# One trunk layer on one core: SSD states by a running scan, and one more pair of blocks by seven products

## The chip, the cores and the metric

The kernel runs on 1 core of one Trainium2 chip. The metric is device microseconds of one execution (us); lower is better. Each time is the median of several runs, and one more execution is profiled. In the profile PE is TensorE's matmuls, PEld its weight loads, DVE is VectorE, ACT ScalarE, POOL GpSimd, and SP the engine that issues most DMAs.

## The reference, cut to what matters

One layer of a hybrid trunk handles 1024 prompt tokens and 8 samples of 16 tokens with shared weights, all in fp32. Chunk-band attention and a Mamba-2 SSD branch share one input projection, and are gated, merged and projected. The change touches the projection's order and the SSD state recurrence:

```python
proj = h @ w_in        # q | k | v | z_att | z_ssd | x,B,C | dt | two merge gates
# per chunk, per SSD head (32 heads of 64 columns, state of 128):
h_new = h * exp(a_cs[:, -1]) + einsum('blgn,blgep->bgepn', bk, xdt * to_end)   # state after the chunk
y_st  = einsum('blgn,bgepn->blgep', ck, h) * exp(a_cs)                         # what the state adds to y
```

The kernel works the prompt in 8 chunks of 128 tokens. State after chunk c = decay(c) times the state after chunk c-1, plus the product of B and the weighted x of chunk c.

## The kernel before, in words

Activations are kept transposed: 128 channels on the partitions, 1152 tokens along the columns. Weights and activations are split into a high and a low part, and each product is three matmuls in fp32r: high by high, high by low, low by high (lines 489, 490, 492). A *block* is 128 output channels of the projection: 8 contraction steps, 3 groups of 384 tokens, 3 matmuls, so 72 matmuls of 384 columns.

The program goes through five stages. (1) The input is loaded and normalised. (2) *Blocks ahead*: the silu gates z of the SSD branch and some merge gates are computed and put into DRAM, the first of them plainly; then NPR *pairs* of blocks are computed together by Strassen's scheme with seven products in the place of eight (`pairs`, lines 880 to 883: 7 forms, 4 contraction steps, 2 halves, 3 matmuls, so 168 matmuls of 288 columns per pair); then one more block plainly. (3) Attention, eight head pairs. (4) The *SSD stage*: 16 head pairs p, in 4 groups. Each pair has a dense part (`conv_gen`, one block, and where `FILL` names the pair a *filler*, which is one further block of z or gate which does not depend on the head pair) and a light part (`prelude` and `main`, many small matmuls with work on DVE, ACT and POOL). (5) The tail: merge gates left over, two branch projections, the output projection.

In `main` of a head pair: x is turned to tokens on the partitions (L1754) and written in two weighted copies, xd and xw (L1758). Eight 128x128 matmuls give B times xw, chunk by chunk, into two PSUM tiles `g` of four chunks (L1799; fp32 matmuls stand as two records each in the trace). ACT copies chunk 0 into `hst` (L1804), and DVE makes the other states in turn, two heads for each of seven chunks (L1808, 14 instructions of 64 columns). Then PE makes the part inside the chunk (L1830), the samples' part (L1837) and the states' part (L1855, which reads `hst` as its weights); DVE adds them up. PSUM has four `g` tiles, two `d`, and one `s` of two banks.

The order in which instructions stand is made by generators and a scheduler: a planner keeps its own clock, adds each generator step's cost, and `pause(t)` holds a generator until the planner's clock has moved t ns. The scheduler then places instructions on each engine, which executes them in that order.

Of the kernel before, what the change touches and what calls it, by code (L numbers as in the profile page):

```python
# [12 lines left out]
P = 128  # L13
# [18 lines left out]
NEARLY = 15  # L32
SLOTS = (('p', 1), ('p', 3), ('p', 6), ('p', 9), ('p', 11), ('p', 13), ('p', 15))
# [5 lines left out]
NPR = 7  # L39
# [92 lines left out]
def trunk_kernel(ctx: ExitStack, tc: tile.TileContext, h):  # L132
# [118 lines left out]
    L_SSD = marena.set_layout(Z0, [("X", 1, XW), ("R", 2, 1184), ("t", 8, 36), ("pad", 1, 576), ("T", 9, NT), ("Y", 1, 1184), ("H", 1, 1024),  # L251
# [1294 lines left out]
    def dt_gen():  # L1546
# [36 lines left out]
        nc.scalar.activation(dec, pe[:, :256], AF.Exp)  # L1583
# [101 lines left out]
    def ssd(p):  # L1685
# [7 lines left out]
        e4 = dec.rearrange("p (c e) -> p c e", e=32)  # L1693
# [43 lines left out]
        def main():  # L1737
# [46 lines left out]
            def masked(q):  # L1784

                t = alloc(L_ST, "x", 2 * P)
                i = 2 * (q % 2)
                nc.gpsimd.tensor_tensor(t.r.rearrange("p (b n) -> p b n", n=P), xs[q // 2].ap.unsqueeze(1).to_broadcast([P, 2, P]),
                                        bmask4[:, i:i + 2].unsqueeze(2).to_broadcast([P, 2, P]), ALU.mult)
                return t  # L1790

            xm = [masked(0), masked(1)]

            yield from pause(1500)
            for j in range(2):
                ps = pg()
                for s in range(4):
                    c = 4 * j + s
                    nc.tensor.matmul(ps[:, s * P:(s + 1) * P], tokb.ap[:, c * P:(c + 1) * P], xw.ap[:, c * P:(c + 1) * P],  # L1799
                                     start=True, stop=True)  # L1800
                for s in range(4):
                    c = 4 * j + s
                    if c == 0:
                        nc.scalar.activation(hst.ap[:, 0:P], ps[:, 0:P], AF.Copy)  # L1804
                        continue
                    for e in range(2):
                        o = c * P + e * HD
                        nc.vector.scalar_tensor_tensor(  # L1808
                            hst.ap[:, o:o + HD], hst.ap[:, o - P:o - P + HD], e4[:, c, 2 * p + e:2 * p + e + 1],
                            ps[:, s * P + e * HD:s * P + e * HD + HD], ALU.mult, ALU.add)  # L1810
                yield 4 * 213
                yield from pause(900)
            xw.free()
# [4 lines left out]
            yield from pause(1200)  # L1818
# [395 lines left out]
```

## Time and profile before

| what | value |
|---|---|
| median of 3 runs | 1942.8 us (1938.79 to 1944.55) |
| the profiled execution | 1943.42 us |
| its span, first to last instruction | 1941.6 us |
| granted TensorE clock | 0.999 |
| busy: PE, DVE, ACT, POOL | 1922.7, 1251.5, 798.3, 339.7 us |
| instructions | 35765 |
| pairs by seven products | 102.2 to 258.7 us of the span |
| SSD stage, first to last of its states' matmuls | 989 to 1504 us |

A matmul's row gives how long it took from start to modelled end. Matmuls overlap in the pipeline, so the rate at which they go is the distance of their starts, and the duration in the row is longer than that. The rows of DVE overlap a little for the same reason.

### The profile page before, as it was taken

What the parts mean: (1) busy time and instruction counts of PE and PEld (TensorE: products, weight loads), DVE (VectorE), ACT (ScalarE), POOL (GpSimd) and SP (SyncE); (2) the same over time, 40 slices, a digit from 0 to 9 for tenths busy, and PEclk for the clock granted to TensorE, in tenths of its full rate; (3) what the DMA queues carried; (4) which work ended last, traced back from release to release, by engine and by line L of the source; (5) the groups of instructions that cost most, each with busy time, mean ns of one, the idle gap of its engine ahead of it and who ended that gap; (6) DMA issues with size and microseconds to landing.
All of it is one profiled execution on the core that took longest, in us unless ns stands there. A gap on an engine that the chain in (4) does not pass through costs nothing.

```text
span 1941.6 us, 35765 instructions
## 1 busy us (share of the span) xinstructions
PE 1922.7 (99%) x14259; PEld 1842.4 (95%) x14259; DVE 1251.5 (64%) x2577; ACT 798.3 (41%) x1639; POOL 339.7 (17%) x615
## 2 busy tenths in 40 slices
PE   7999999999999999999999999999999999999999
PEld 5999999999899998998999999999999999999999
DVE  6756634555556456558597988888885434777732
ACT  7533324444454444545655546465453311111200
POOL 0000003213123131221022343242241300000000
PEclk9999999999999999999999999999999999999999
DMA  8222342343333333423345354554558742331341
GB/s 316 92 81 95 109 173 69 96 129 116 97 117 101 122 116 94 130 82 115 119 132 181 132 162 152 168 173 140 160 192 289 292 144 93 105 105 56 89 143 52
DMA packets 85966, 258.73 MB, mean 133 GB/s; under 512 B 14732, under 2 KB 15768, under 8 KB 85800
## 3 DMA queue, kind: packets, MB, share of 16 engines
q1 hardware_dynamic: 77416, 229.57, 36.5%
q0 software_dynamic: 8384, 26.88, 3.6%
q8 instruction: 112, 1.84, 0.4%
q14 instruction: 54, 0.44, 0.1%
HBM read 202.72 MB, written 53.68 MB: 132 GB/s over the span
## 4 chain that ended last, share of the span: by engine, by line
PE 92%; DVE 3%; DMA 2%; ACT 1%; issue 1%; POOL 0%; SPq 0%; ACTq 0%; DVEq 0%; POOLq 0%
PE d L489 11%; PE d L492 11%; PE d L490 11%; PE d L557 5%; PE d L555 5%; PE d L556 5%; PE s L489 4%; PE s L490 4%; PE s L492 4%; PE g L1311 3%; PE g L1334 3%; PE s L1390 2%; PE g L880 2%; PE g L883 2%; PE g L882 2%; PE g L490 1%
## 5 line engine op out<-in xcount | busy, mean ns | idle before, releaser
L489 PE MATMUL d<-rarena 128*128 128x384 f32 x1288 | 437.7, 340 | 0.0
L492 PE MATMUL d<-rarena 128*128 128x384 f32 x1288 | 434.2, 337 | 0.0
L490 PE MATMUL d<-rarena 128*128 128x384 f32 x1288 | 433.3, 336 | 0.0
L489 PEld LDWEIGHTS d<-rarena 128*128 128x128 f32 x1288 | 242.0, 188 | 4.1 <-issue 2.7
L492 PEld LDWEIGHTS d<-rarena 128*128 128x128 f32 x1288 | 241.9, 188 | 2.2 <-issue 2.0
L490 PEld LDWEIGHTS d<-rarena 128*128 128x128 f32 x1288 | 242.1, 188 | 0.8 <-issue 0.4
L557 PE MATMUL d<-va_att,rarena 128*128 128x384 f32 (+1 forms) x567 | 197.6, 349 | 0.0
L555 PE MATMUL d<-va_att,rarena 128*128 128x384 f32 (+1 forms) x567 | 196.7, 347 | 0.0
L556 PE MATMUL d<-va_att,rarena 128*128 128x384 f32 (+1 forms) x567 | 193.7, 342 | 0.0
L374 ACT ACTIVATE rarena<-arena 128x1024 fp32r<-128x1024 f32 x76 | 80.5, 1059 | 262.9 <-PE s L490 173.9
L489 PE MATMUL s<-rarena 128*128 128x384 f32 x488 | 165.6, 339 | 0.0
L490 PE MATMUL s<-rarena 128*128 128x384 f32 x488 | 164.2, 336 | 0.0
L492 PE MATMUL s<-rarena 128*128 128x384 f32 x488 | 163.3, 335 | 0.0
L1299 ACT ACTIVATE ma_att<-ma_att 128x640 f32<-128x640 f32 (+2 forms) x144 | 101.5, 706 | 135.8 <-DVE ma_att L1408 99.7
L1228 POOL TENSOR_SCALAR ma_att<-ma_att 128x16 f32<-128x16 f32 (+1 forms) x24 | 5.2, 218 | 707.3 <-DVE ma_att L1205 417.2
L557 PEld LDWEIGHTS d<-va_att,rarena 128*128 128x128 f32 x567 | 107.0, 189 | 3.9 <-issue 2.7
L555 PEld LDWEIGHTS d<-va_att,rarena 128*128 128x128 f32 x567 | 106.8, 188 | 2.7 <-issue 1.2
L375 DVE TENSOR_TENSOR rarena<-arena,rarena 128x1024 fp32r<-128x1024 f32 x76 | 93.3, 1227 | 22.6 <-ACT rarena L374 22.6
L556 PEld LDWEIGHTS d<-va_att,rarena 128*128 128x128 f32 x567 | 106.8, 188 | 0.5
L1531 DVE SCALAR_TENSOR_TENSOR ma_att<-ma_att,arena 128x1176 f32<-128x1176 f32 x63 | 93.9, 1491 | 9.4 <-ACT ma_att L1528 8.1
L489 PEld LDWEIGHTS s<-rarena 128*128 128x128 f32 x488 | 91.7, 188 | 1.3 <-issue 1.2
L490 PEld LDWEIGHTS s<-rarena 128*128 128x128 f32 x488 | 91.7, 188 | 0.8 <-issue 0.8
(437 smaller groups left out, 4128.0 us busy)
## 6 DMA issues: line engine op xcount, KB each, us to landing
arena<-in_wall_dram SPq DMA_DIRECT2D x85, 512.0 KB, 3.6
ma_att<-in_kc_dram SPq DMA_DIRECT2D x64, 256.0 KB, 4.3
ma_att<-in_vc_dram SPq DMA_DIRECT2D x64, 256.0 KB, 3.5
ma_att<-acs_d SPq DMA_DIRECT2D x23, 576.0 KB, 6.8
ma_att<-y_d SPq DMA_DIRECT2D x15, 576.0 KB, 6.3
arena<-in_wssd_dram SPq DMA_DIRECT2D x16, 512.0 KB, 4.5
z_d<-va_start SPq DMA_DIRECT2D x13, 576.0 KB, 2.8
ma_att<-eacs_d SPq DMA_DIRECT2D x26, 288.0 KB, 3.9
```

The lines of the kernel that those rows point to most:

```text
L374: keep(nc.scalar.activation(hi.r[:, c], b.ap, AF.Copy))
L375: keep(nc.vector.tensor_tensor(lo.r[:, c], b.ap, hi.ap[:, c], ALU.subtract))
L489: nc.tensor.matmul(ps, hi.r[:, wc], kh.r[:, tok], start=k == 0, stop=False)
L490: nc.tensor.matmul(ps, hi.r[:, wc], kl.r[:, tok], start=False, stop=False)
L492: nc.tensor.matmul(ps, lo.r[:, wc], kh.r[:, tok], start=False, stop=k == nk - 1)
L555: nc.tensor.matmul(ps, kh.r[:, tok], wh, start=j == 0, stop=False)
L556: nc.tensor.matmul(ps, kh.r[:, tok], wl, start=False, stop=False)
L557: nc.tensor.matmul(ps, kl.r[:, tok], wh, start=False, stop=j == KT - 1)
L1299: nc.scalar.activation(p, p, AF.Exp, bias=sm_[:, 4 + e:5 + e], scale=-1.0, accum_out=sm_[:, 6 + e:7 + e])
L1311: nc.tensor.transpose(ps[:, s * P:(s + 1) * P], p[:, (j + s) * P:(j + s + 1) * P], ident)
L1334: late(nc.tensor.matmul(po[e * HD:e * HD + HD, a * P:(a + 1) * P], v.ap[:, vc:vc + HD], x.ap[:, o + i * P:o + (i + 1) * P], start=i == 0, ...
L1531: nc.vector.scalar_tensor_tensor(yc, r.ap[:, j:j + n], w4[:, i, j:j + 1], yc, ALU.mult, ALU.add)
```

## The change

Three things are edited.

**States by a scan.** In `main`, all eight state matmuls go to two PSUM tiles that are taken at once. ACT copies both into `xw` (whose content those matmuls have just read), with the chunk as the innermost index: 8 chunks of one column lie side by side. ACT also spreads the decays of one head over a new buffer `dd` of 512 columns (`decays`). One `tensor_tensor_scan` of DVE per head (512 columns: 64 columns by 8 chunks) runs the recurrence in place; the decay of chunk 0 is set to zero once in `dt_gen`, which starts each column anew. ACT then copies the states out of `xw` into `hst`, whose order is as before, chunk outermost, one copy per head. The 14 instructions of L1808 and the copy of L1804 are gone.

**Eight pairs in the place of seven.** NPR goes from 7 to 8 and NEARLY, the number of z or gate blocks after the first four gates that are computed ahead, from 15 to 17. The block z14, which was the plain one after the pairs, and z15 make the eighth pair, and gate 4 is now the plain block.

**Five fillers in the place of seven.** z15 and gate 4 stood in the SSD stage with head pairs 1 and 3. The five blocks that stay (gates 5 to 9) stand with head pairs 1, 3, 6, 10 and 15. The number of blocks overall is the same.

```diff
-NEARLY = 15
-SLOTS = (('p', 1), ('p', 3), ('p', 6), ('p', 9), ('p', 11), ('p', 13), ('p', 15))
+NEARLY = 17
+SLOTS = (('p', 1), ('p', 3), ('p', 6), ('p', 10), ('p', 15))
-NPR = 7
+NPR = 8
...
-        nc.scalar.activation(dec, pe[:, :256], AF.Exp)
+        d8 = dec.rearrange("p (e c) -> p e c", c=8)
+        nc.scalar.activation(d8, pe[:, :256].rearrange("p (c e) -> p e c", e=32), AF.Exp)
+        nc.vector.memset(d8[:, :, 0], 0.0)
...
+            dd = yield from walloc(lay, "D", 8 * HD)
+
+            def decays(e):
+                nc.scalar.activation(dd.ap[:, :8 * HD].rearrange("p (d c) -> p d c", c=8),
+                                     e4[:, 2 * p + e].unsqueeze(1).to_broadcast([P, HD, 8]), AF.Copy)
+
+            decays(0)
             yield from pause(1500)
+            ps2 = [pg(), pg()]
+            for c in range(8):
+                nc.tensor.matmul(ps2[c // 4][:, c % 4 * P:(c % 4 + 1) * P], tokb.ap[:, c * P:(c + 1) * P], xw.ap[:, c * P:(c + 1) * P],
+                                 start=True, stop=True)
+            xc = xw.ap[:, :NP].rearrange("p (n c) -> p n c", c=8)
             for j in range(2):
-                ps = pg()
-                for s in range(4):
-                    c = 4 * j + s
-                    nc.tensor.matmul(ps[:, s * P:(s + 1) * P], tokb.ap[:, c * P:(c + 1) * P], xw.ap[:, c * P:(c + 1) * P],
-                                     start=True, stop=True)
-                for s in range(4):
-                    c = 4 * j + s
-                    if c == 0:
-                        nc.scalar.activation(hst.ap[:, 0:P], ps[:, 0:P], AF.Copy)
-                        continue
-                    for e in range(2):
-                        o = c * P + e * HD
-                        nc.vector.scalar_tensor_tensor(
-                            hst.ap[:, o:o + HD], hst.ap[:, o - P:o - P + HD], e4[:, c, 2 * p + e:2 * p + e + 1],
-                            ps[:, s * P + e * HD:s * P + e * HD + HD], ALU.mult, ALU.add)
-                yield 4 * 213
+                nc.scalar.activation(xc[:, :, 4 * j:4 * j + 4], ps2[j].rearrange("p (c n) -> p n c", n=P), AF.Copy)
+            yield 8 * 213
+            yield from pause(1000)
+            hc = hst.ap[:, :NP].rearrange("p (c n) -> p n c", c=8)
+            for e in range(2):
+                hv = xw.ap[:, e * HD * 8:(e + 1) * HD * 8]
+                nc.vector.tensor_tensor_scan(hv, dd.ap[:, :8 * HD], hv, 0.0, ALU.mult, ALU.add)
+                if e == 0:
+                    decays(1)
+                nc.scalar.activation(hc[:, e * HD:(e + 1) * HD], xc[:, e * HD:(e + 1) * HD], AF.Copy)
                 yield from pause(900)
+            dd.free()
             xw.free()
...
-            yield from pause(1200)
+            yield from pause(0)
```

Three places show how the order moves. A row names the line, the operation, what it writes and reads, and the shape; g, d and s are PSUM tiles, rarena holds split weights and activations, ma_att and va_ssd are the two working areas in SBUF.

PE, at the end of the seventh pair. Before, the plain block follows:

```order
L883 MATMUL g_867<-rarena 128x288
L880 MATMUL g_868<-rarena 128x288
L882 MATMUL g_868<-rarena 128x288
L883 MATMUL g_868<-rarena 128x288
L489 MATMUL d_2354<-rarena 128x384
L490 MATMUL d_2354<-rarena 128x384
L492 MATMUL d_2354<-rarena 128x384
```

Of the change, at the same place:

```order
L883 MATMUL g_867<-rarena 128x288
L880 MATMUL g_868<-rarena 128x288
L882 MATMUL g_868<-rarena 128x288
L883 MATMUL g_868<-rarena 128x288
L880 MATMUL g_865<-rarena 128x288
L882 MATMUL g_865<-rarena 128x288
L883 MATMUL g_865<-rarena 128x288
```

168 more matmuls of 288 columns stand here, and 144 of 384 columns fewer in the SSD stage.

DVE, in the light part of head pair 12 (the first of the last group). Before, L1808 makes the states, L1758 the weighted copies ahead of it, L1531 is a convolution, L375 a weight split, and L1848 adds the skip part:

```order
L1758 TENSOR_TENSOR ma_att<-g_14248,ma_att 128x128 x2
L1808 SCALAR_TENSOR_TENSOR va_ssd<-va_ssd,ma_att,g_14264 128x64 x2
L1781 TENSOR_TENSOR rarena<-ma_att,rarena 64x128
L1808 SCALAR_TENSOR_TENSOR va_ssd<-va_ssd,ma_att,g_14264 128x64 x4
L375 TENSOR_TENSOR rarena<-arena,rarena 128x1024
L1808 SCALAR_TENSOR_TENSOR va_ssd<-va_ssd,ma_att,g_14296 128x64 x3
L1531 SCALAR_TENSOR_TENSOR ma_att<-ma_att,arena 128x1176
L1808 SCALAR_TENSOR_TENSOR va_ssd<-va_ssd,ma_att,g_14296 128x64 x2
L1848 SCALAR_TENSOR_TENSOR ma_att<-ma_att,arena,g_14347 128x512
L1531 SCALAR_TENSOR_TENSOR ma_att<-ma_att,arena 128x1176
L1848 SCALAR_TENSOR_TENSOR ma_att<-ma_att,arena,g_14356 128x512
L1808 SCALAR_TENSOR_TENSOR va_ssd<-va_ssd,ma_att,g_14296 128x64 x2
```

Of the change (L1816 is the scan, which this view names like L1808; L1857 is the old L1848, L1783 the old L1781):

```order
L1760 TENSOR_TENSOR ma_att<-g_14295,ma_att 128x128 x2
L1531 SCALAR_TENSOR_TENSOR ma_att<-ma_att,arena 128x1176
L1783 TENSOR_TENSOR rarena<-ma_att,rarena 64x128
L1816 SCALAR_TENSOR_TENSOR va_ssd<-ma_att,va_ssd 128x512
L375 TENSOR_TENSOR rarena<-arena,rarena 128x1024
L1857 SCALAR_TENSOR_TENSOR ma_att<-ma_att,arena,g_14401 128x512
L1816 SCALAR_TENSOR_TENSOR va_ssd<-ma_att,va_ssd 128x512
L1537 SCALAR_TENSOR_TENSOR ma_att<-ma_att 128x1024
L1857 SCALAR_TENSOR_TENSOR ma_att<-ma_att,arena,g_14410 128x512
```

Fourteen short instructions in six places became two, and no state instruction reads PSUM any more.

ACT, same head pair. Before (L1804 copies the first state, L1727 is the prelude of the pair after):

```order
L1508 ACTIVATE ma_att<-d_14337 128x384
L1804 ACTIVATE va_ssd<-g_14264 128x128
L1780 ACTIVATE rarena<-ma_att 64x128
L374 ACTIVATE rarena<-arena 128x1024
L1511 ACTIVATE ma_att<-s_14410 128x256
L1512 ACTIVATE ma_att<-s_14410 128x8x16
L1144 ACTIVATE va_ssd<-g_14278 96x384
L1528 ACTIVATE ma_att<-ma_att,arena 128x1176
L1727 ACTIVATE va_ssd<-va_ssd,ma_att 128x128 x9
```

Of the change (L1810 copies a PSUM tile into xw, L1798 spreads the decays, L1819 copies states to hst):

```order
L1810 ACTIVATE va_ssd<-g_14310 128x128x4
L1810 ACTIVATE va_ssd<-g_14311 128x128x4
L374 ACTIVATE rarena<-arena 128x1024
L1511 ACTIVATE ma_att<-s_14442 128x256
L1512 ACTIVATE ma_att<-s_14442 128x8x16
L1533 ACTIVATE ma_att<-ma_att 128x1176
L1798 ACTIVATE ma_att<-ma_att 128x512
L1819 ACTIVATE va_ssd<-va_ssd 128x64x8
L1144 ACTIVATE va_ssd<-g_14334 96x384
L1819 ACTIVATE va_ssd<-va_ssd 128x64x8
```

The way from the state matmuls to `hst` now goes through ACT, DVE, ACT, DVE and ACT again, with a weight split's copy (L374) and an activation of the convolution (L1533) between.

More of the change, by code (lines that the diff above doesn't have):

```diff
@@ L250, in trunk_kernel @@
     L_ATT["Z"] = L_ATT["T"][2:]
-    L_SSD = marena.set_layout(Z0, [("X", 1, XW), ("R", 2, 1184), ("t", 8, 36), ("pad", 1, 576), ("T", 9, NT), ("Y", 1, 1184), ("H", 1, 1024),
+    L_SSD = marena.set_layout(Z0, [("X", 1, XW), ("R", 2, 1184), ("t", 8, 36), ("D", 1, 576), ("T", 9, NT), ("Y", 1, 1184), ("H", 1, 1024),
                                   ("g", 3, G3)])
@@ L1692, in ssd @@
         w4 = dtw.rearrange("p (c e) -> p c e", e=32)
-        e4 = dec.rearrange("p (c e) -> p c e", e=32)
+        e4 = dec.rearrange("p (e c) -> p e c", c=8)
         s4 = decs.rearrange("p (b e) -> p b e", e=32)
```

## The prediction

> **What bounds the kernel now.** I read the page's busy shares and the chain of waits first, then PE's waits, then the rows of PE's timeline for its rate, then stage windows, and last one head pair of the SSD stage.
>
> ```profile
> PE 1922.7 (99%) x14259; PEld 1842.4 (95%) x14259; DVE 1251.5 (64%) x2577; ACT 798.3 (41%) x1639; POOL 339.7 (17%) x615
> ...
> PE 92%; DVE 3%; DMA 2%; ACT 1%; issue 1%; POOL 0%; SPq 0%; ACTq 0%; DVEq 0%; POOLq 0%
> ```
>
> PE is busy for 99% of the span and carries 92% of the chain that ends last. So time is won only by giving PE less to do or by taking away one of its waits. PE's waits are few:
>
> ```profile
> PE g L634 <- DMA m<-in_xT_dram: 8.5, 2, 8.3
> PE g L1881 <- POOL rarena L1788: 2.1, 2, 1.2
> PE g L1675 <- DVE ma_att L1537: 1.4, 1, 1.4
> ...
> PE g L1830 <- DVE ma_att L1808: 0.7, 1, 0.7
> ...
> PE g L1855 <- DVE ma_att L1848: 0.2, 1, 0.2
> ```
>
> The 8.5 us are the load of the input at the start, which nothing here touches. The other four stand in the SSD stage and make 2.1 + 1.4 + 0.7 + 0.2 = 4.4 us. That is all that this stage can give back by shorter waits, and only the 0.7 us name an instruction that the change removes.
>
> What PE pays for a block is read from the starts of matmuls in undisturbed rows:
>
> ```profile
> 92.12 0.33 PE L492 MATMUL d<-rarena 128*128 128x384 f32 x1
> ...
> 98.36 0.33 PE L492 MATMUL d<-rarena 128*128 128x384 f32 x1
> ```
>
> ```profile
> 253.76 0.30 PE L880 MATMUL s<-m,rarena 128*128 128x288 f32 x1
> ...
> 258.55 0.29 PE L880 MATMUL g<-rarena 128*128 128x288 f32 x1
> ```
>
> Between the first two lie 36 matmuls: 6.24 / 36 = 0.1733 us for 384 columns. Between the others, also 36: 4.79 / 36 = 0.1331 us for 288 columns.
>
> The SSD stage has the other engines most loaded. The first row is the sixth pair by seven products, the others the SSD stage (stretch, length, then PE, PEld, DVE, ACT, POOL busy):
>
> ```profile
> 214.00:236.30 22.30, 22.30 (x169) 22.30 (x168) 13.73 (x24) 7.05 (x15) 0.00 (x0) 1.00 0.30 101
> ...
> 940.00:1100.00 160.00, 158.57 (x1272) 155.06 (x1270) 128.62 (x225) 88.31 (x188) 37.62 (x65) 1.00 0.47 150
> 1100.00:1250.00 150.00, 150.00 (x1141) 146.95 (x1141) 134.75 (x217) 83.50 (x174) 51.37 (x84) 1.00 0.47 152
> 1250.00:1400.00 150.00, 149.01 (x1142) 145.15 (x1143) 127.46 (x219) 79.03 (x164) 48.61 (x80) 1.00 0.48 155
> 1400.00:1520.00 120.00, 117.95 (x924) 115.96 (x921) 82.26 (x142) 48.53 (x103) 34.44 (x57) 1.00 0.75 256
> ```
>
> From 940 to 1520 us DVE is busy for 128.6 + 134.8 + 127.5 + 82.3 = 473 us of 580, or 82%, and up to 90% in the second row; ACT for 299 us, or 52%. PE is still the bound there, but DVE has little to spare, and dense blocks are what PE does while DVE works.
>
> **The change part by part.** *The eighth pair.* Two plain blocks are 144 matmuls: 144 x 0.1733 = 24.96 us. The pair is 168 x 0.1331 = 22.36 us (the seven pairs fill 102.2 to 258.7 us, 156.5 / 7 = 22.36, the same). PE gains 2.60 us. DVE and ACT work 13.7 and 7.1 us in a pair's 22.3 us, so PE bounds it: I cost this work at nothing, and without that cover it would be some 21 us. The loads and stores of the two blocks move with them, in a stretch where the DMA engines are busy 0.30 of the time: nothing. The sums of weights that the pair makes ahead are in the 13.7 us.
>
> *The fillers.* Two blocks leave the SSD stage, and PE's work there falls by 24.96 us, from about 580 to 555 us. This costs nothing as long as DVE and ACT keep up, so their new load has to be worked out.
>
> *DVE.* What it had for the states, and the nearest rows to what it gets:
>
> ```profile
> L1808 DVE SCALAR_TENSOR_TENSOR ma_att<-ma_att,g 128x64 f32<-128x64 f32 x168 | 35.7, 273 | 4.8 <-ACT ma_att L1804 2.6 <-PE g L1799 2.0
> ...
> L1808 DVE SCALAR_TENSOR_TENSOR va_ssd<-va_ssd,ma_att,g 128x64 f32<-128x64 f32 x56 | 12.2, 274 | 0.9 <-PE g L1799 0.8
> ...
> L1890 DVE TENSOR_TENSOR qa_ssd<-qa_ssd,g 128x512 f32<-128x512 f32 x16 | 10.9, 679 | 5.2 <-PE g L1881 5.1
> ...
> L1871 DVE TENSOR_TENSOR qa_ssd<-qa_ssd,ma_att 128x1024 f32<-128x1024 f32 x8 | 9.7, 1218 | 0.0
> ```
>
> L1808 is busy for 35.7 + 12.2 = 47.9 us, 3.0 us per head pair. The trace has no scan. Below, it is an operation of two inputs over 512 columns, 0.68 us (L1890); above, I let it go like 1024 columns, 1.22 us (L1871), since a recurrence may take a second cycle per element. Two scans are 1.4 to 2.4 us, so DVE gains 1.6 to 0.6 us per head pair, 26 to 10 us in all, and some 3 us more with the weight splits of the two blocks. Its share in the stage becomes (473 - 29) / 555 = 80%, or (473 - 13) / 555 = 83%. So DVE's load per PE time is about what it was: what the scan takes off pays for the two fillers, and no more. I take the upper price, as the recurrence is a dependence that L1890 does not have.
>
> [...]
>
> *ACT.* The nearest rows are copies of 1024 columns, of 512 from PSUM, of 512 from SBUF, and the old copy of the first state:
>
> ```profile
> L374 ACT ACTIVATE rarena<-arena 128x1024 fp32r<-128x1024 f32 x76 | 80.5, 1059 | 262.9 <-PE s L490 173.9 <-issue 44.1 <-PE g L490 42.2
> ...
> L1313 ACT ACTIVATE ma_att<-g 128x512 f32<-128x512 f32 x96 | 54.8, 591 | 13.7 <-PE g L1311 13.1
> ...
> L812 ACT ACTIVATE rarena<-qa_start 128x512 fp32r<-128x512 f32 x21 | 13.2, 627 | 18.0 <-PE s L882 18.0
> ...
> L1804 ACT ACTIVATE ma_att<-g 128x128 f32<-128x128 f32 x12 | 3.3, 274 | 15.9 <-PE g L1799 10.8 <-DMA out_hs_dram<-ma_att 5.1
> ```
>
> Six new activations per head pair: 2 x 0.59 + 4 x 0.63 - 0.27 = 3.4 us at the pace of contiguous rows. If steps of 32 or 512 bytes cost them as much as 1024 columns, 6 x 1.06 - 0.27 = 6.1 us. ACT goes from 299 us to 354 or 397 us of 555, 64 to 72%. It keeps up on average; I take the lower, as no row here shows a copy that pays for its stride, and keep the upper for the range.
>
> *The chain to hst.* PE must not reach L1855's matmuls before the states are in `hst`. In head pair 12 before:
>
> ```profile
> 1398.42 1.05 PE L1799 MATMUL g<-va_ssd 128*128 128x128 f32 x8
> ...
> 1407.04 1.05 PE L1855 MATMUL g<-ma_att,va_ssd 128*128 128x128 f32 x8
> ```
>
> ```profile
> 1407.83 0.27 DVE L1808 SCALAR_TENSOR_TENSOR va_ssd<-va_ssd,ma_att,g 128x64 f32<-128x64 f32 x1
> ```
>
> The last state (which only goes out) was made 8.6 us after the last state matmul. In the new order ACT stands in a row for this pair with two copies (1.18), L374 (1.06), two evictions (0.6), L1533 (1.2), decays (0.63), a copy to `hst` (0.63), an eviction (0.5) and the second copy (0.63): 6.4 us; the second scan falls beside it. PE has, between its last state matmul and the first use, 24 dense matmuls (4.2 us), the small products of L1830 (18 instructions, some 2 us) and L1837 and L1142 (1 us each): 8 us. It fits by 1.6 us. Head pair 8 has the least between, 11 dense matmuls (1.9 us) and the same small products, 5.9 us; its chain is 1.18, the scan 1.22, decays 0.63, a scan 1.22 and a copy 0.63, 4.9 us at my prices, and with all six activations at 1.06 it is 2.12 + 1.22 + 1.06 + 1.22 + 1.06 = 6.7 us, 0.8 us late. So new waits are bounded by nothing below and about 0.8 us in each of 16 pairs, 13 us, above. I take nothing: most pairs have 25 or more dense matmuls between.
>
> *What is freed.* The two `g` tiles were held until DVE had read them in the midst of its other work; ACT now empties them in 1.2 us. The 0.7 us of L1830 on L1808 go. The other 3.7 us of waits name POOL's products and DVE's convolution, which stay. The zeroing of decays and the turned exponential happen once, under dense work: nothing.
>
> *The sum*, against the profiled execution's own 1943.42 us (span 1941.6 and 1.8 around it): 1943.4 - 2.6 - 0.7 = 1940.1 us. That execution is 0.6 us above the median, so I predict 1939.5 us, 0.2% less.
>
> **The rivals.** *All waits of the SSD stage go too.* If a shorter DVE queue brings L1537 and the operands of L1788 in time, all 4.4 us go: 1942.8 - 2.6 - 4.4 = 1935.8 us. For it: 1.4 us are a wait on DVE. Against it: 2.1 us are POOL's, which the change leaves alone, and DVE's share stays near 82%. Chance 0.30.
>
> *The chain to hst is late (slower).* The place is PE's first L1855 in each head pair, behind which every dense matmul in PE's order waits. If strided copies of ACT cost as 1024 columns or more and queue behind L374 and L1533, `hst` comes after PE: with 1 us late in each of 16 pairs, 16 us, 1955 us. It decides from the point where the six activations cost about 1 us each in the tight pairs. For it: five hops across two in-order queues in the place of a DVE run, and PE's order leaves only 6 to 8 us in some pairs. Against it: 8.6 us was the old length. Chance 0.14.
>
> [...]
>
> *Fewer blocks, same stage.* DVE at 83% with uneven load may hold PE for what the eighth pair won: PE's waits in the stage rise by 3 us or so, and the time stays 1943 us. For it: 134.75 of 150 us in one stretch already. Against it: those very stretches have no PE wait now. Chance 0.10.
>
> **How the numbers follow.** My forecast has 0.46. A difference under 0.3% (5.8 us) is what a measurement of this kernel can't tell from no change. Same: the forecast (0.42 of its 0.46) and the third rival, 0.52. Faster: the first rival and the forecast's edge, 0.34. Slower: the second rival, 0.14. The range goes from 1935.8 less some 3 us of the runs' own spread, 1933, to the forecast with 9 of the 13 us of late states, 1949.
>
> **What would show it.** The pairs' matmuls should run on for 22.4 us more, to about 281 us, with attention unchanged and 22 us later. The scans should last 0.7 to 1.2 us, the copies 0.6 us. PE's waits after 940 us should sum to 3 to 5 us. A wait of PE at the L1855 matmuls on ACT's copies, or copies near 1.1 us, would make the slower rival right; a wait on L1537 or the dense evictions would make the third right; no waits past 940 us, the first.

## The result, and the profile after

| | before | after |
|---|---|---|
| median | 1942.5 us (1938.8 to 1944.6, 5 runs) | 1964.2 us (1962.3 to 1969.7, 5 runs) |
| profiled execution, span | 1943.42, 1941.6 us | 1963.65, 1961.9 us |
| granted TensorE clock | 0.999 | 0.997 |
| busy: PE, DVE, ACT, POOL | 1922.7, 1251.5, 798.3, 339.7 us | 1926.4, 1252.7, 862.8, 328.4 us |

The change is slower: the ratio to before is 1.0116, with a 95% interval from 1.0099 to 1.0133. Forecast were 1939.5 us, and a range up to 1949.

The eighth pair went as worked out. The row of L883 after (duration, then first and last start):

```profile
L883 PE MATMUL g<-rarena x192: 293/295/298, 101.2 to 279.8; 128*128 128x288 f32 x192
```

Before, the last start of this row was at 258.8 us. What follows the pairs thus begins 21.0 us later, and has 24.96 us of dense matmuls less to do, so the span should have ended at 1941.6 + 21.0 - 25.0 = 1937.6 us. It ended at 1961.9. So some 24 us were lost behind the pairs. PE's waits after, those of more than 1 us:

```profile
PE g L1890 <- POOL rarena L1790: 10.0, 10, 1.9
PE g L634 <- DMA m<-in_xT_dram: 8.3, 1, 8.3
PE g L1864 <- ACT va_ssd L1819: 4.3, 4, 2.1
PE g L1864 <- ACT ma_att L1819: 4.3, 3, 2.4
PE g L1756 <- DVE ma_att L1537: 1.9, 1, 1.9
```

L1890 (before L1881) multiplies POOL's masked products; L1864 (before L1855) reads `hst`. The first row was 2.1 us before, and waits of L1855 on ACT's copies did not exist. I also took the distance of the starts of neighbouring matmuls over the usual distance of the same two lines. From 980 us on, excesses over 0.25 us sum to 24 to 29 us after and some 7 us before, by whether the median or a low quantile is taken as usual: 17 to 22 us more stalls. Some 5 us more are matmuls at half the clock, in three stretches of 3.41 us at a granted 0.50 (last section): two begin at a wait of L1864 on ACT's copies, one at a wait of L1890 on POOL. Together that is about the loss, and by PE's waits those for `hst` and those for POOL's products have a like share in it.

Why POOL's products are late is seen one engine further back. DVE's waits in the SSD stage after:

```profile
DVE ma_att L1870 <- DMA ma_att<-eacs_d: 42.3, 11, 7.1
DVE va_ssd L1870 <- DMA va_ssd<-eacs_d: 17.1, 5, 6.3
```

All 16 head pairs wait, 59.4 us in all. L1870 multiplies by `eb`, the exponentials that are broadcast from DRAM (`eacs_d`); before, the same waits of L1861 were:

```profile
DVE va_ssd L1861 <- DMA va_ssd<-eacs_d: 2.9, 1, 2.9
DVE ma_att L1861 <- DMA ma_att<-eacs_d: 1.6, 2, 1.2
```

One head pair in order of time (start, duration, engine, line; idle time before it in brackets), from the timelines of DVE, ACT, SP, POOL and PE after:

```profile
1078.24 1.22 DVE L1816 TENSOR_TENSOR_SCAN ma_att<-ma_att 128x512 f32<-128x512 f32 x1
...
1079.49 1.16 ACT L1819 ACTIVATE ma_att<-ma_att 128x512 f32<-128x512 f32 x1 [1.49 <-DVE ma_att L1816]
...
1080.68 1.09 SPq L1825 DMA_DIRECT2D ma_att<-eacs_d  x2
...
1081.63 1.22 DVE L1880 TENSOR_TENSOR qa_ssd<-qa_ssd,ma_att 128x1024 f32<-128x1024 f32 x1
1089.22 1.35 DVE L1870 TENSOR_TENSOR ma_att<-ma_att,g 128x384 f32<-128x384 f32 x3 [6.38 <-DMA ma_att<-eacs_d]
...
1091.76 1.22 DVE L1537 SCALAR_TENSOR_TENSOR ma_att<-ma_att 128x1024 f32<-128x1024 f32 x1
...
1093.03 0.10 POOL L1500 MEMSET ma_att<- 128x3 f32 x1 [11.55 <-DVE ma_att L1537]
...
1098.16 2.31 POOL L1790 TENSOR_TENSOR rarena<-rarena,arena 128x256 fp32r<-128x256 f32 x2
...
1098.82 0.51 PE L1890 MATMUL g<-rarena 128*128 128x256 f32 x2 [1.57 <-POOL rarena L1790]
```

`eb` takes the place of `xw` in SBUF. Before, the last reader of `xw` was PE's state matmuls. Now the states themselves live in `xw` until ACT's second copy has taken them out, at 1079.49 + 1.16 = 1080.65; the load is issued 0.03 us later, and L1870 starts 8.5 us after that. DVE has two short instructions left to start ahead of L1870 (L1857, not shown, and L1880) and then stands for 6.4 us. Behind it are the convolution (L1537), POOL's instructions on it, POOL's store and products, and PE.

SP's longest waits before this load say the same of the two kernels, before and after:

```profile
SPq L1816 <- PE g L1799: 15.9, 8, 5.3
```

```profile
SPq L1825 <- ACT ma_att L1798: 21.4, 11, 4.2
SPq L1825 <- ACT ma_att L1819: 15.7, 3, 6.5
SPq L1825 <- ACT va_ssd L1819: 9.9, 2, 6.9
```

The first of the three names the wrong instruction: L1798 stands behind the second copy in ACT's order and ended after the load was issued. In each of the 16 pairs the issue begins 0.02 to 0.07 us after the end of the second copy.

`hst` itself is late too. In head pair 8, from the same timelines:

```profile
1290.96 1.05 PE L1806 MATMUL g<-va_ssd 128*128 128x128 f32 x8
...
1294.72 1.07 ACT L1810 ACTIVATE va_ssd<-g 128x512 f32<-128x512 f32 x2
1295.83 1.23 DVE L1816 TENSOR_TENSOR_SCAN va_ssd<-ma_att,va_ssd 128x512 f32<-128x512 f32 x1 [0.71 <-ACT va_ssd L1810]
...
1297.75 1.22 DVE L1816 TENSOR_TENSOR_SCAN va_ssd<-ma_att,va_ssd 128x512 f32<-128x512 f32 x1
1299.00 1.10 ACT L1819 ACTIVATE va_ssd<-va_ssd 128x512 f32<-128x512 f32 x1 [0.31 <-DVE va_ssd L1816]
1300.16 2.08 PE L1864 MATMUL g<-ma_att,va_ssd 128*128 128x128 f32 x10 [2.09 <-ACT va_ssd L1819]
```

From the end of the last state matmul to the end of the second copy are 8.1 us here; over the 16 pairs 5.5 to 12.3 us, with a median of 7.5. The longest ones stand behind other work in the queues of ACT and DVE: here the first copy begins 2.7 us after the state matmuls, in ACT's order behind L374, L1640 and L1533.

### The profile page after: what moved, and what is told of

It is laid out like the page before. It is cut to its first block, busy times and chain, and to the rows that moved or that the text cites. A ratio compares the mean times of both kernels' runs of the same rounds, so it can differ in the third digit from the quotient of the medians.

```text
span 1961.9 us, 35729 instructions
## 1 busy us (share of the span) xinstructions
PE 1926.4 (98%) x14283; PEld 1842.7 (94%) x14283; DVE 1252.7 (64%) x2402; ACT 862.8 (44%) x1725; POOL 328.4 (17%) x609
## 5 line engine op out<-in xcount | busy, mean ns | idle before, releaser
L489 PE MATMUL d<-rarena 128*128 128x384 f32 x1256 | 427.6, 341 | 0.0
L492 PE MATMUL d<-rarena 128*128 128x384 f32 x1256 | 423.9, 338 | 0.0
L490 PE MATMUL d<-rarena 128*128 128x384 f32 x1256 | 423.7, 337 | 0.0
L489 PEld LDWEIGHTS d<-rarena 128*128 128x128 f32 x1256 | 236.7, 188 | 3.0 <-issue 2.4
L492 PEld LDWEIGHTS d<-rarena 128*128 128x128 f32 x1256 | 236.8, 189 | 1.1 <-issue 0.9
L490 PEld LDWEIGHTS d<-rarena 128*128 128x128 f32 x1256 | 236.7, 188 | 0.8 <-issue 0.4
L374 ACT ACTIVATE rarena<-arena 128x1024 fp32r<-128x1024 f32 x74 | 78.3, 1059 | 240.4 <-PE s L490 156.7
L489 PE MATMUL s<-rarena 128*128 128x384 f32 x472 | 160.8, 341 | 0.0
L490 PE MATMUL s<-rarena 128*128 128x384 f32 x472 | 159.0, 337 | 0.0
L492 PE MATMUL s<-rarena 128*128 128x384 f32 x472 | 158.9, 337 | 0.0
L375 DVE TENSOR_TENSOR rarena<-arena,rarena 128x1024 fp32r<-128x1024 f32 x74 | 91.3, 1234 | 21.4 <-ACT rarena L374 21.1
L1531 DVE SCALAR_TENSOR_TENSOR ma_att<-ma_att,arena 128x1176 f32<-128x1176 f32 x63 | 93.5, 1484 | 5.6 <-ACT ma_att L1528 4.3
L489 PEld LDWEIGHTS s<-rarena 128*128 128x128 f32 x472 | 89.0, 189 | 1.1 <-issue 1.0
L490 PEld LDWEIGHTS s<-rarena 128*128 128x128 f32 x472 | 89.0, 189 | 0.2 <-issue 0.2
```

Of the source, the lines that this page charges most:

```text
L374: keep(nc.scalar.activation(hi.r[:, c], b.ap, AF.Copy))
L375: keep(nc.vector.tensor_tensor(lo.r[:, c], b.ap, hi.ap[:, c], ALU.subtract))
L489: nc.tensor.matmul(ps, hi.r[:, wc], kh.r[:, tok], start=k == 0, stop=False)
L490: nc.tensor.matmul(ps, hi.r[:, wc], kl.r[:, tok], start=False, stop=False)
L492: nc.tensor.matmul(ps, lo.r[:, wc], kh.r[:, tok], start=False, stop=k == nk - 1)
L1531: nc.vector.scalar_tensor_tensor(yc, r.ap[:, j:j + n], w4[:, i, j:j + 1], yc, ALU.mult, ALU.add)
```

## The experiments

**Theory A**: `eb` comes late because it takes the place of `xw`, DVE stands for it in its order, and PE pays. **Theory B**: the chain to `hst` got longer (ACT's copies of 1.12 us), and PE waits for it. **Theory C**: two fillers too few. The diff also takes away a pause of 1200 behind the load and adds one of 1000; no run changes these two alone. Ratios are to the kernel before, run beside each, with 95% intervals.

### The two halves of the change

`scan_only` has the new states, with the numbers of pairs and fillers of before; `blocks_only` has the new numbers and the old states.

```diff
 # scan_only, against the change
-NEARLY = 17; SLOTS = (('p', 1), ('p', 3), ('p', 6), ('p', 10), ('p', 15)); NPR = 8
+NEARLY = 15; SLOTS = (('p', 1), ('p', 3), ('p', 6), ('p', 9), ('p', 11), ('p', 13), ('p', 15)); NPR = 7
 # blocks_only is the reverse edit of the kernel before
```

> The scan as in the change, but seven pairs and seven fillers as before. Theory A (the states now live in xw's place until ACT has copied them out, so the load of the decays eb, which takes that place, comes late; DVE stands at the product with eb, in the changed kernel 59 us in 16 waits, and convolution, POOL's products and PE wait behind it): about the changed kernel's time or a little less, since the fillers give more cover, 1953 to 1967 us, with 40 us or more of DVE waits on eacs_d. Theory B (the chain to hst itself is late, through the copies out that take 1.12 us each): the same time, 1953 to 1967 us, with most of PE's waits at L1864's like. Theory C (the loss is from the two missing fillers): 1943 us within 4.

> Eight pairs and five fillers, but states as before by L1808's instructions, no scan. Theories A and B: the eighth pair's 2.6 us are won and not much lost, 1936 to 1944 us. Theory C (the fillers' cover is missing): 1955 us or more, PE waits in the SSD stage of 15 us or more.

Measured: scan_only 1956.5 us, 1.0073 [1.0051, 1.0096]; blocks_only 1944.2 us, 1.0008 [0.9999, 1.0018]. The states alone cost some 14 us, with all seven fillers there, so theory C alone is out. DVE's waits for `eb` are 43.5 us in scan_only, as theory A expected; L1864 waits for the copies 4.7 us of PE's 12.1, a share and not most of it, as B had expected. The blocks alone do not gain their 2.6 us. The longest of PE's waits in blocks_only are:

```profile
PE g L1881 <- POOL rarena L1788: 4.4, 2, 4.2
PE g L1855 <- DVE ma_att L1848: 1.4, 2, 0.7
```

By this profile one wait of 4.2 us for POOL's products took it, and 6.8 us at half the clock behind it (the mean granted clock from 1428 to 1436 us was 0.57). The two halves sum to 15.1 us, the whole change to 21.7. That the late chain of the scan shows more without the two fillers would fit, and no run separates it.

### The late load alone

`late_eb` is the kernel before with one small copy per head pair. It computes nothing that is used, and keeps `xw` busy until the last state. It has a second effect: ACT stands in its order for DVE's last state, 20.8 us in all before these copies.

```diff
+            nc.scalar.activation(xw.ap[:, :1], hst.ap[:, 8 * P - 1:8 * P], AF.Copy)
             xw.free()
             eb = alloc(lay, "T", NT)
```

> The kernel before, with one added instruction per pair: ScalarE copies the last column of the states into one column of xw before xw is freed, so that eb's load can start only when the state chain is done, as in the change. Nothing else of the change is in it. Theory A (eb's late load holds VectorE, and that costs TensorE): VectorE's waits for eacs_d grow from 4.5 us to 25 us or more, TensorE's waits for GpSimd's masked products from 2.4 us to 6 us or more, and the time rises by 5 to 12 us, to 1948 to 1955 us. Theory B (only the longer chain to hst costs): the chain to hst is the old one here, so the time stays within 2 us of 1942.8 us. The added copy itself is 16 times some 0.2 us on ScalarE, which is not the bound.

Measured: 1956.7 us, 1.0069 [1.0052, 1.0086], 12.8 us over the 1943.9 us of before beside it. DVE's and PE's waits in late_eb:

```profile
DVE ma_att L1862 <- DMA ma_att<-eacs_d: 41.0, 12, 5.5
DVE va_ssd L1862 <- DMA va_ssd<-eacs_d: 13.8, 3, 5.9
```

```profile
PE g L1754 <- DVE va_ssd L1537: 2.7, 1, 2.7
PE g L1754 <- DVE ma_att L1862: 1.8, 1, 1.8
PE g L1754 <- DVE ma_att L1537: 1.4, 2, 0.9
PE g L1882 <- POOL rarena L1788: 1.3, 1, 1.3
```

With no scan, no copies out and all fillers, the late load costs about what scan_only costs, and there is no stretch at half the clock in its SSD stage (granted 1.00 on average in each of four stretches from 962 to 1542 us). DVE's waits came as theory A expected; the time is 1.7 us above its range of 1948 to 1955. The place where PE pays was another: here it is mostly L1754, the transposes of the next pair, and not POOL's products (6 us or more were expected). Since ACT stands too, 12.8 us are the price of both, and no run has the load late without that. Theory B as the only cause is out, since `hst` is not changed here; its share in the change is not priced by this run.

### eb in another place, and other copies

`eb_slot` frees `xw` and takes `eb` only after `me` and `xd` are free. `contig_out` turns the two copies out so that they write contiguous columns and read in steps of 32 bytes.

```diff
 # eb_slot
-            xw.free()
-            eb = alloc(lay, "T", NT)   # and its two DMAs
...
             for t in me + [xd]:
                 t.free()
+            eb = alloc(lay, "T", NT)   # and its two DMAs
+            xw.free()
 # contig_out
-                nc.scalar.activation(hc[:, e * HD:(e + 1) * HD], xc[:, e * HD:(e + 1) * HD], AF.Copy)
+                nc.scalar.activation(hst.ap[:, :NP].rearrange("p (c n) -> p c n", c=8)[:, :, e * HD:(e + 1) * HD],
+                                     xw.ap[:, :NP].rearrange("p (n c) -> p c n", c=8)[:, :, e * HD:(e + 1) * HD], AF.Copy)
```

> The changed kernel, but xw is given back after the decay matrices me and xd, and eb is allocated after them, so eb's load waits for PE's L1839 products and not for the copies out. Theory A: DVE's waits on eacs_d fall from 59 us to under 20 us, and the time to 1940 to 1952 us. Theory B: PE's waits on the copies out stay at 8 us or more and the time stays at 1960 to 1966 us.

> The changed kernel, but the copies out to hst go through their elements with the column innermost: they write side by side and read with a step of 32 bytes, where the change writes with a step of 512 bytes. If the step of the writes is what makes them 1.12 us, they go to 0.63 us. Theory B then: 1948 to 1957 us, PE's waits on these copies from 8.6 us to under 3 us. Theory A: each eb load starts 0.5 to 1 us earlier and DVE's waits on eacs_d fall by 8 to 16 us of 59, 1956 to 1962 us. If reads with a step cost the same, nothing moves.

Measured: eb_slot 1954.7 us, 1.0063 [1.0047, 1.0079]; contig_out 1968.9 us, 1.0127 [1.0102, 1.0152]. eb_slot gives back 9.5 of 21.7 us. It still starts the load late, only behind other work: DVE waits 34.6 us in the first multiplies. Theory A had expected under 20 us and 1940 to 1952 us, theory B 1960 to 1966 us; the waits on the copies fell to 5.8 us, and the run fits neither alone. contig_out's copies are no faster:

```profile
L1819 ACT ACTIVATE ma_att<-ma_att 128x512 f32<-128x512 f32 x18 | 21.2, 1176 | 3.2 <-DVE ma_att L1816 3.2
```

They took 1124 ns in the change. So 512 single elements read 32 bytes apart (1176 ns) took about as long as 512 written 512 bytes apart (1124 ns). This run did not shorten the chain and tells nothing for or against B.

### An earlier chain, a later multiply, an eb in two pieces

Three cheap ways to let the load catch up: `early_chain` drops the pauses around the state matmuls, `late_multiply` gives the multiply a later due time, `split_eb` loads `eb` into `xw` in two pieces.

```diff
 # early_chain
-            yield from pause(1500)
             ps2 = [pg(), pg()]
...
             yield 8 * 213
-            yield from pause(1000)
 # late_multiply
-            te, tz = clock[0] + 4000, clock[0] + 6500
+            te, tz = clock[0] + 9000, clock[0] + 11500
 # split_eb, inside the loop over e, after the copy of head e
+                ce = slice(e * 512, 512 if e == 0 else NT)
+                for i in range(2):
+                    dma(xw.ap[i * HD:(i + 1) * HD, ce], eacs_d[hds[i]:hds[i] + 1, ce].to_broadcast([HD, ce.stop - ce.start]))
...
-            xw.free()
-            eb = alloc(lay, "T", NT)
+            eb = xw
```

> The change with the state matmuls and the scan issued 2.5 us earlier in the planner's time (both pauses around the state matmuls dropped). Theory B (chain to hst late): the waits of the inter-chunk matmuls for the copies fall from 8.6 us to under 3 us, and eb's load is earlier by up to 2.5 us, so VectorE's waits on eacs_d fall from 59 us to about 25 us; the time falls by 8 to 14 us, to 1950 to 1956 us. If what matters is the engines' load and not the delay, it stays within 3 us of 1964 us.

> The change with the multiply by eb given 5 us more in VectorE's order (due 9 us after the pair's own matmuls and not 4), so that other work of VectorE stands ahead of it while eb's load runs. Nothing else differs. Theory A (the wait hurts because VectorE runs its queue in order): VectorE's waits for eacs_d fall from 59 us to under 20 us, the masked products come on time, TensorE's stalls fall by about 10 us, and the time is 1948 to 1956 us. If it is VectorE's load and not the order: within 3 us of 1964 us. A risk: the results in PSUM are held 5 us longer, which can hold back matmuls instead.

> The change with eb loaded straight into xw, in two pieces by columns: the first 512 columns as soon as the first head's copy has left them, the rest after the second head's copy. The scan, the copies, pairs and fillers are those of the change. Theory A: the first multiply by eb needs only the first piece, which starts some 3 us earlier; VectorE's waits for eacs_d fall from 59 us to about 20 us, TensorE's waits for the masked products from 10 us to about 4 us, and the time to 1950 to 1958 us. The waits of the inter-chunk matmuls for the copies (8.6 us) stay. If eb's load doesn't matter: 1962 to 1970 us.

Measured: early_chain 1985.3 us, 1.0214 [1.0194, 1.0233]; late_multiply 1966.2 us, 1.0125 [1.0105, 1.0145]; split_eb 1966.9 us, 1.0124 [1.0109, 1.0140]. early_chain missed every time that was expected. The other two missed theory A's times and came where the other reading had them: within 3 us of 1964, and 1962 to 1970. The traces say why for two of the three.

late_multiply did not do what it says. Between the last scan and the first multiply stood 5.5 instructions of DVE (median of 16) in the change and 5 here, and the waits for the load were 55.6 us: the later due time put nothing in between, so this run does not test what it was made for. In early_chain the multiply still waited for the load, 54.8 us, and now held the PSUM tiles that the next pair's transposes need:

```profile
PE g L1756 <- DVE ma_att L1868: 20.4, 7, 6.7
PE g L1862 <- ACT ma_att L1817: 8.2, 5, 3.4
```

A pause is a place in an order, not a length: without it the consumers moved up too. The granted clock of early_chain is lower too, 0.990 on average and 0.997 in the change. In split_eb the first multiplies waited for the load 29.3 us in the place of 59.4, and the second ones 13.8 us in the place of none. With these 16 us PE's waits for POOL's products halved, from 10.0 to 5.0 us, but the transposes (L1756) now waited 4.1 us for the multiply, and PE's waits past the pairs grew from 21 to 24 us. So less waiting of DVE for `eb` does not by itself shorten the time. Why the waits moved stays open, and the run counts against a theory A that is the whole cause.

### eb early, and no copies

`no_copy` loads `eb` at the start of the pair into the place of `hst`, and PE reads the states as weights from `xw`, 8 elements apart. `no_copy_7` is the same with seven pairs and seven fillers.

```diff
-            hst = yield from walloc(lay, "T", NP)
+            eb = yield from walloc(lay, "T", NT)   # and its two DMAs
...
-                nc.scalar.activation(hc[:, e * HD:(e + 1) * HD], xc[:, e * HD:(e + 1) * HD], AF.Copy)
...
-                        nc.tensor.matmul(p2[:, s * P:(s + 1) * P], hst.ap[:, (k - 1) * P:k * P], ct.ap[:, k * P:(k + 1) * P],
+                        nc.tensor.matmul(p2[:, s * P:(s + 1) * P], xc[:, :, k - 1], ct.ap[:, k * P:(k + 1) * P],
```

> The change without the two copies per pair out of the scan's layout (32 times 1.12 us of ScalarE): TensorE reads the states as weights from the scan's own layout, a step of 8 elements apart, and only the last state is copied (128 elements) for its output. hst's buffer is gone, so eb takes it and its load starts before the pair's chain. Theory A and B together: both the late eb (16 waits of VectorE, 59 us in all) and the copies that the inter-chunk matmuls wait for (8.6 us) are gone; TensorE's stalls fall from 27.5 us to about 10 us, and with the throttle's 5 us gone the time is 1940 to 1946 us. A alone: the waits on eacs_d go and the waits of the inter-chunk matmuls stay at 5 us or more. Theory C (two fillers too few): no better than 1955 us. Open: a strided weight read may cost TensorE time; if each of the 112 costs 0.1 us, 11 us.

> As no_copy, but with seven Strassen pairs and seven fillers as before. If the fillers matter only where VectorE and ScalarE are late, it is 2.6 us above no_copy by the saved products of one pair; if the fillers are needed anyway (blocks_only lost 4 us of its 2.6 us gain), it is level with or 1 to 3 us below no_copy: 1939 to 1944 us.

Measured: no_copy 1963.3 us, 1.0101 [1.0079, 1.0122]; no_copy_7 1967.6 us, 1.0121 [1.0104, 1.0138]. The waits went as A and B together expected. Of PE's waits past the pairs in no_copy, 3.1 us in all, the longest is:

```profile
PE g L1758 <- DVE va_ssd L1762: 1.0, 1, 1.0
```

But the strided weights, which I had left open with 11 us, cost more. Weight loads in no_copy, and the same of before:

```profile
L1860 PEld LDWEIGHTS g<-va_ssd,ma_att 128*128 128x128 f32 x98 | 24.3, 333 | 0.8 <-PE g L1842 0.7
```

```profile
L1855 PEld LDWEIGHTS g<-ma_att 128*128 128x128 f32 x112 | 14.3, 191 | 0.4 <-DVE ma_att L1848 0.3
```

A load takes 333 ns in the place of 191. From each of the 224 rows of these matmuls to PE's next start are 50.5 us in no_copy and 23.6 us before: 26.9 us more. Without them no_copy would be at about 1936 us. That is a subtraction and not a run; the next kernel tests it. As it stands the time lies in the range of theory C, but no_copy_7, with all seven fillers, is not faster: it lies 4.3 us over no_copy, which the 2.6 us of the eighth pair and the intervals allow.

### eb early, the copies late

`copy_late` keeps the early `eb`, and copies the states out into a new `hst` right after the pair's own matmuls have freed `xd`. `copy_late_fill7` has the fillers of before beside it, with eight pairs.

```diff
 # against no_copy
             for t in me + [xd]:
                 t.free()
+            hst = alloc(lay, "T", NP)
+            hc = hst.ap[:, :NP].rearrange("p (c n) -> p n c", c=8)
+            for e in range(2):
+                nc.scalar.activation(hc[:, e * HD:(e + 1) * HD], xc[:, e * HD:(e + 1) * HD], AF.Copy)
+            store(h["out_hp"][p], hst.ap[:, 7 * P:])
+            xw.free()
```

> The change with eb loaded early, into the place that hst had, and hst allocated only after the pair's own matmuls, in the place of xd; the two copies of 1.12 us stand there, right before the inter-chunk matmuls, and the weights are contiguous again (no 27 us as in no_copy). Theory A (eb's late load is the main cost): VectorE's waits for eacs_d are 0, and the time falls by 10 us or more, to 1938 to 1952 us, below eb_slot (1954.7). Theory B (the copies' delay is as costly): the inter-chunk matmuls now wait 1 to 2 us for the copies in most of the 16 pairs, 15 to 30 us in all, and the time stays at 1955 to 1970 us.

> As copy_late, with seven fillers in place of five (eight Strassen pairs, two blocks more out of the last stretch). By the two runs of pairs (blocks_only 1944.2, pairs8_fill7 1940.4) 1 to 5 us below copy_late; if the copies are hidden, 1936 to 1942 us and level with or below pairs8_fill7.

Measured: copy_late 1947.0 us, 1.0021 [1.0012, 1.0031]; copy_late_fill7 1946.2 us, 1.0016 [1.0006, 1.0026]. No multiply waits for `eb` any more, and 17.1 of the 21.7 us are back, with the scan, the eight pairs and the five fillers as they were. The copies still take 1.12 us, stand as near to PE's use as can be, and cost little. Since the edit takes away both the late load and most of the waits for `hst`, 17.1 us are the price of the two together; no run takes either alone out of the change. copy_late_fill7 lies 0.8 us lower, which the intervals do not tell apart (1 to 5 us were expected). The longest of PE's waits in copy_late:

```profile
PE d L489 <- ACT ma_att L1640: 4.6, 1, 4.6
PE g L1865 <- ACT va_ssd L1848: 1.7, 2, 1.2
...
PE g L1865 <- ACT ma_att L1848: 0.9, 1, 0.9
```

So the waits for `hst` are 2.6 us in this order. In the change they were 8.6 us, and two of the three stretches at half the clock began at them, which costs some 3.4 us more. The 1936 us of the subtraction are missed by 11 us: PE's waits are 10.5 us in the place of 3.1, and 6.8 us at half the clock behind the longest of them cost some 3.4 us (dense matmuls of 384 columns start 0.32 us apart from 1467.64 us on, 0.17 us apart ahead of the wait). That largest wait, 4.6 us for the eviction of a gate block, is the same kind of thing on ACT, whose queue stood for another load at that place:

```profile
1459.25 5.37 ACT L1729 ACTIVATE ma_att<-ma_att 128x128 f32<-128x128 f32 x18 [10.29 <-DMA ma_att<-acs_d]
...
1466.64 0.46 ACT L1640 ACTIVATE ma_att<-d 128x384 f32<-128x384 f32 x1
```

### The part that pays

`pairs8_fill7` is the kernel before with eight pairs and all seven fillers; two blocks more come out of the last stretch.

```diff
-NEARLY = 15
+NEARLY = 17
-NPR = 7
+NPR = 8
```

> The kernel before with eight Strassen pairs and still seven fillers, at the same seven places; the two blocks more come out of the last stretch, where all blocks are plain. If blocks_only lost its 2.6 us to the two missing fillers (one wait of 4.2 us for GpSimd's masked products and 3.5 us of halved clock behind it), this one keeps it: 1940 to 1941.5 us, 1.5 to 3 us below the kernel before. If the loss is in the eighth pair itself, it is level with blocks_only, 1943.5 to 1945 us.

Measured: 1940.4 us, 0.9987 [0.9978, 0.9996], 2.3 us below before: faster than both kernels, and level with the 2.6 us of the eighth pair. In its profile, PE's waits behind the pairs:

```profile
PE g L1881 <- POOL rarena L1788: 1.1, 1, 1.1
PE g L1855 <- DVE ma_att L1848: 0.6, 2, 0.4
```

Beside blocks_only (1.0008, interval from 0.9999) this shows that the two fillers are worth their places in the SSD stage, some 3.7 us, with the old states. With the new ones copy_late and copy_late_fill7 show no such difference.

## Why the prediction was wrong, step by step

- *The eighth pair, 2.6 us.* Right. The pairs shifted the rest by 21.0 us (22.4 forecast; the first pair also began 1.4 us earlier), and pairs8_fill7 has the gain as a time.
- *The chain to hst, "I take nothing" for new waits.* This is the step that failed, in two ways. The first is a term that was set to nothing: L1864 does wait for the copies, 8.6 us in 7 of 16 pairs, and the half clock behind two of these waits costs some 3.4 us more. The sum is within the bound of 13 us that I kept, but not by the working of it: the chain was forecast at 4.9 us in head pair 8 and 6.4 in head pair 12, and took 8.1 and 8.5. I had added up the instructions of the chain, with some of what stood beside them, and not the time that they stand in two busy queues. The second was not in the working at all. I followed `hst` to its reader and did not follow `xw` to its next tenant. The line `xw.free()` stays where it was in the diff, but the last reader of `xw` ahead of it is now ACT's second copy and no longer PE's state matmuls, and the load of `eb` hangs on that. late_eb prices such a lateness at 12.8 us in the kernel before, with ACT's standing in it; taking both out of the change gives back 17.1 us. How the loss of the change divides between the two stays open. The new reads and writes of `xw` were in the diff, and SP's row on L1799 was in the trace of before.
- *The fillers, "costs nothing as long as DVE and ACT keep up".* On average they keep up: DVE is busy for 457 of the 580 us from 962 to 1542 us, 79%, ACT for 355 us, 61%. The share was the wrong test. DVE lost 59 us of standing in its order, not for lack of time, and blocks_only loses 4.2 us at one place.
- *DVE's scan at the upper price.* Right: 1221 ns forecast as 1.22 us. A scan of 512 columns took as long as L1871's operation on 1024 before (1218 ns); why it does, no run shows.

```profile
L1816 DVE TENSOR_TENSOR_SCAN ma_att<-ma_att 128x512 f32<-128x512 f32 x22 | 26.9, 1221 | 8.4 <-ACT ma_att L1810 5.8 <-ACT ma_att L1798 2.4
```

- *ACT's six activations at the lower price.* Right for four, wrong for two:

```profile
L1798 ACT ACTIVATE ma_att<-ma_att 128x512 f32<-128x512 f32 x32 | 20.1, 629 | 12.4 <-DVE ma_att L1816 8.8 <-DVE va_ssd L1816 3.0 <-PE g L1334 0.6
L1810 ACT ACTIVATE ma_att<-g 128x512 f32<-128x512 f32 x22 | 11.9, 594 | 11.8 <-PE g L1806 11.8
...
L1819 ACT ACTIVATE ma_att<-ma_att 128x512 f32<-128x512 f32 x18 | 20.2, 1124 | 3.9 <-DVE ma_att L1816 3.9
```

  The copies out, which write single elements, cost 1.12 us and not 0.63; the upper price had been taken for all six. Per head pair that makes 2 x 0.63 + 2 x 0.59 + 2 x 1.12 - 0.27 = 4.4 us, 1.0 us over the forecast, and all of it in the chain.
- *What is freed, 0.7 us.* The wait of L1830 on the states is gone, but POOL's and the convolution's waits, put down as "which stay", grew from 3.5 to 11.9 us.
- *The rivals.* The slower one had the right sign and one right mechanism, the wait at L1855's matmuls on ACT's copies, at a chance of 0.14. Its price of 16 us was twice the 8.6 us measured there, or 12 with the clock behind it, and the rest of the loss had another cause. The third rival, a time of 1943 us with some 3 us more of waits, is about what blocks_only shows with the old states: 1944.2 us, and 7.4 us of PE's waits in the place of 4.4. PE's waits past 940 us, forecast at 3 to 5 us, were 21 us. No rival held that a load is late, and none had the clock.

## What to carry to other kernels

When an edit lengthens the life of a buffer, look up who takes its place next: here the new tenant's load was issued 0.02 to 0.07 us after the end of the new last reader, and DVE stood 59.4 us for it, with the convolution, POOL's products and PE behind it. DVE's busy share of 79% said nothing about that; the wait rows of the queue that issued the load did: SP's longest ahead of it were 15.9 us on PE before and 47.0 us on ACT after. When a result passes through several queues, add the time that each step stands in its queue to the time that it takes: in head pair 8 the steps were forecast at 4.9 us, and the way took 8.1. And a small copy that holds a buffer longer, put into the kernel before, gives a price for such a delay in one run, before anything is rebuilt; the engine that makes the copy can stand for it too (ACT for 20.8 us in late_eb), which belongs to the price.

## What the runs showed of the hardware that I had not expected

**In the change, three waits of PE of 1.9 to 2.4 us were each followed by 3.41 us at half the clock.** Stretches of 3.41 us in the profile after; the first three rows that show a clock of 1.00 are each followed by a stretch at 0.50, of which one is shown, and the fourth by one at 1.00 (start:end, length, then PE, PEld, DVE, ACT, POOL busy, granted clock):

```profile
1297.25:1300.66 3.41, 1.32 (x33) 1.23 (x31) 3.35 (x4) 2.98 (x4) 0.26 (x1) 1.00 0.26 101
1300.66:1304.07 3.41, 3.41 (x16) 3.41 (x16) 1.68 (x4) 0.00 (x0) 0.56 (x3) 0.50 0.66 223
1362.10:1365.51 3.41, 1.01 (x7) 0.69 (x5) 3.41 (x4) 2.31 (x4) 0.00 (x0) 1.00 0.04 4
...
1447.43:1450.84 3.41, 1.43 (x8) 1.22 (x9) 1.39 (x2) 3.41 (x11) 3.16 (x7) 1.00 0.00 0
...
1095.87:1099.28 3.41, 1.84 (x10) 1.35 (x9) 3.41 (x4) 0.84 (x1) 3.41 (x4) 1.00 0.53 155
1099.28:1102.69 3.41, 2.21 (x14) 2.17 (x14) 3.35 (x4) 1.29 (x3) 3.39 (x4) 1.00 0.41 148
```

The change has three stretches at half the clock in the SSD stage, behind waits of 2.1, 2.4 and 1.9 us, and some 5 us of its loss are theirs; before had none there. Their starts are 64.85 and 85.33 us apart, which is 19 and 25 times the 3.413 us that each of them lasts. With the SSD stage divided into steps of that length from their starts, PE was busy, in the step just ahead of each, for 1.01 to 1.43 of 3.41 us; the least busy step of the stage that was not followed by half the clock had 1.84 us. So in this run it was not the length of one wait that told them apart but how much of it fell into one step: another wait of 1.9 us, at 1032 us, lies across two steps, with PE busy for 2.36 and 2.58 us, and nothing follows. Over the runs there is no sharp point: in contig_out a step with 1.56 us of PE was followed by half the clock once and once not, and in split_eb one with 2.17 us was. The 4.2 us wait of blocks_only filled a whole step and was followed by two at half the clock, some 3.4 us of loss. What lowers the clock, and at which idle time, is not shown by these runs.

**512 single fp32 elements apart took ACT 1124 and 1176 ns in the place of 629, and strided weight loads 333 ns in the place of 191.** In the change, 512 elements per partition took 629 ns where ACT wrote them side by side (L1798) and 594 ns where it wrote runs of four from PSUM (L1810), 1124 ns where it wrote single elements 512 bytes apart, and in contig_out 1176 ns where it read single elements 32 bytes apart. A weight load of 128 columns took 333 ns with a step of 32 bytes (no_copy) and 191 ns without (before). Why a step costs this, no run shows.
